# A transformer trunk on one core: first loads in smaller pieces over two queues, and three groups of work asked for later

## The chip, the cores and the metric

The kernel runs on one core of a Trainium2 chip. Its engines are named as the profile names them: PE (TensorE, the matmuls; PEld is its loading of weights), ACT (ScalarE), DVE (VectorE), POOL (GpSimd) and SP (SyncE, which issues most DMAs). Each takes its own list of instructions in order; semaphores hold an instruction until what it needs is there. The metric is the device time of one execution in microseconds (us).

## The reference

Two layers work on x, 256 positions of 1024 features. What matters here, cut from the reference:

```python
for l in range(DEPTH):                                   # DEPTH = 2
    x = x + 0.5 * swiglu(rmsnorm(x, ffn1_norm[l]), ffn1_w_gate[l], ffn1_w_up[l], ffn1_w_down[l])
    h = rmsnorm(x, mix_norm[l])
    proj = h @ w_in[l]                                   # q, k, v, xr, yr, cq and three gates
    ...
    br_attn = window_attention(q, k, v, attn_sinks[l]) @ w_attn_out[l]
    br_lru = rglru_branch(xr, yr, conv_w[l], conv_b[l], ...) @ w_lru_out[l]
    br_mem = memory_attention(cq, rmsnorm(mem, mem_norm[l]), w_mem_kv[l]) @ w_mem_out[l]
    merged = g[:, :, 0] * br_attn + g[:, :, 1] * br_lru + g[:, :, 2] * br_mem
    x = x + merged @ w_out[l]
    x = x + 0.5 * swiglu(rmsnorm(x, ffn2_norm[l]), ffn2_w_gate[l], ffn2_w_up[l], ffn2_w_down[l])
return rmsnorm(x, final_norm)
```

`rglru_branch` begins with a causal convolution of four taps along the positions, `xc[s] = conv_b + sum over d of conv_w[3-d] * xr[s-d]`; two gates come from products of `xc` with blocks of 64 x 64, through sigmoids.

## The kernel before

x lies feature-major in one buffer, eight tiles of 128 features x 256 positions. All weights were packed in the order of their use, in blocks of 128 x 128; eight blocks are a slab (128 x 1024 floats, 512 KB), 432 slabs in all. SP loads each slab into one of five stage buffers `st`. So that fp32 products can be made of fast ones, a slab is split: ACT makes the rounded high half `whi` (line 194), DVE the rest `wlo = st - whi` (line 195). Activations are split in the same way (`xs`, `h`, `xcs`). A block takes two matmuls: the high half against both halves of the activation, 512 columns (line 219), and the low half against the high one, 256 columns (line 220). The PSUM tiles of the pool `mm` have three buffers; each holds a pair of output tiles, and a later pair gets a buffer when the copies and sums that read it are done: ACT copies one half out, and one step later DVE adds the other (`join`, line 256).

The order of the lists is the order in which the Python code issues, and the code counts steps: when `block` (line 198) begins a slab, it first prepares slabs up to three ahead (`prep`: load, `whi`, `wlo`) and then calls `tick`, which runs all tasks that are due. `at(delay, f)` puts `f` into that list, `delay` slabs later. So a delay decides behind which other rows a task stands in the list of its engine, not when it runs.

`start` (line 384) issues nine warm-up matmuls on zeros, the loads of x (pairs of tiles), of the first five slabs and of the constants, then splits x times the norm's gain (`hi` on ACT or DVE at line 414 and 416, `lo` at line 324) and the first four slabs in pieces. The first norm needs the sum of squares over all features: ACT squares pairs of tiles (line 331), DVE adds them to `acc` (line 343), two matmuls `stat` against ones give the sums per position (line 284), nine small DVE rows make the reciprocal root `r` (lines 288 to 298), and two matmuls `rst` (line 305) spread it over the partitions. `n0.then(6, 8)` asks for `stat` at step 6 and `rst` at step 8. The first FFN products run on x without that factor, which is multiplied in later. `mem_norm` does the same for the memory tokens in layer 0: squares from step 5, `stat` and `rst` at steps 11 and 14 of its own count.

`mix` makes the projections pair by pair: `xr` (four pairs, tiles `pxr`), `kv` (`pkv`), q (`pq`, two pairs) and cq (`pcq`, two pairs), and behind each of the last four the products of the recurrent gates (`lg`, `lru_gates`). For each pair of `xr`, `conv` asks for the first tap on ACT (`first`, line 650, step 3), for the other three taps of each tile on DVE (`others`, line 654, steps 4 and 5) and for the split into `xcs` (ACT at step 6, DVE at step 7). The pairs are counted 0 to 3. `lru_gates` issues four sigmoids on ACT and the product `gi` on DVE (line 682). The first sigmoid behind other functions needs a table load.

Of the kernel before, what the change touches and what calls it, by code (L numbers as in the profile page):

```python
# [19 lines left out]
F32 = mybir.dt.float32  # L20
F32R = mybir.dt.float32r
I32 = mybir.dt.int32
AF = mybir.ActivationFunctionType
ALU = mybir.AluOpType
# [5 lines left out]
KT = D // 128  # L30
# [64 lines left out]
class Trunk:  # L95
# [288 lines left out]
    def start(self):  # L384
        nc = self.nc
        warm = self.sm("warm")
        nc.gpsimd.memset(warm, 1.0)
        nc.scalar.activation(warm, warm, AF.Silu)
        zero = self.s1("zero")
        nc.vector.memset(zero, 0.0)  # L390
        ps = self.att("warm")
        for _ in range(9):
            nc.tensor.matmul(ps[:, 0:128], zero[:, 0:128], zero[:, 128:256], start=True, stop=True)
        self.pk = self.pc.tile([128, NVEC], F32, name="pk")
        g = self.pk[:, 0:8]
        self.x = self.big("x")
        n0 = self.Norm(self, "ffn1_norm", 0)
        self.cst = self.pc.tile([128, 640], F32, name="cst")
        self.ones, self.ident, self.dist = self.cst[:, 0:128], self.cst[:, 128:256], self.cst[:, 256:640]
        ld = lambda p: nc.sync.dma_start(self.x[:, 2 * p:2 * p + 2, :], self.xT[:, 2 * p:2 * p + 2, :])  # L400
        ld(0)
        nc.scalar.dma_start(g, self.pkd[:, 0:8])
        for p in range(4):
            list(self.load(2))
            if p < 3:
                ld(p + 1)
        list(self.load())
        nc.sync.dma_start(self.cst, self.constd)
        nc.sync.dma_start(self.pk[:, 8:], self.pkd[:, 8:])

        for p in range(4):
            for k in (2 * p, 2 * p + 1):
                if k % 2:
                    nc.vector.tensor_scalar(n0.xs.hi(k), self.x[:, k, :], g[:, k:k + 1], None, op0=ALU.mult)
                else:
                    nc.scalar.activation(n0.xs.hi(k), self.x[:, k, :], AF.Copy, scale=g[:, k:k + 1])
            n0.lo_tiles(self.x, 2 * p, 2)
            list(self.prep(4 if p == 0 else 2))
        for p in range(4):
            self.at(1, n0.square, self.x, p)  # L420
            self.at(1 + p // 2, n0.add)
        n0.then(6, 8)
        return n0

# [47 lines left out]
    def mem_norm(self):  # L472

        n = self.Norm(self, "mem_norm", 0, split=False)
        self.load_mem()
        for p in range(4):
            self.at(5 + p, n.square, self.mem, p)
            self.at(6 + p, n.add)

        def b():  # L480
            self.Rm = self.pc.tile([128, 256], F32, name="Rm")
            self.rstd_b(n.r, self.Rm)

        self.at(11, n.a)
        self.at(14, b)

    def mem_split(self, l):
        m = self.mem
# [141 lines left out]
    def mix(self, l, norm, nxt):  # L630
        nc, V, A, G = self.nc, self.nc.vector, self.nc.scalar, self.nc.gpsimd
# [4 lines left out]
        xr, xc = self.big("xr"), self.big("xc")  # L636
        xcs = Halves(self, "xcs")

        def project(dst, ps):
            mult = lambda: V.tensor_tensor(dst, dst, norm.R2, op=ALU.mult)  # L640
            self.join(dst, ps, lambda: norm.when(mult))

        def conv(p, ps):
            project(xr[:, sl(p), :], ps)
            xq = slice(2 * p, 2 * p + 2)
            tap = lambda c, i: self.vec("conv_w", l, 8 * i + c)

            def first():
                for c in (2 * p, 2 * p + 1):
                    A.activation(xc[:, c, :], xr[:, c, :], AF.Identity, scale=tap(c, 3), bias=self.vec("conv_b", l, c))  # L650

            def others(c):
                for d in (1, 2, 3):
                    V.scalar_tensor_tensor(xc[:, c, d:], xr[:, c, :256 - d], tap(c, 3 - d), xc[:, c, d:],
                                           op0=ALU.mult, op1=ALU.add)

            self.at(3, first)
            self.at(4, others, 2 * p)
            self.at(5, others, 2 * p + 1)
            self.split(xc[:, xq, :], xcs, 2 * p, 2, delay=6)  # L660

        for p in range(4):
            conv(p, self.pair("pxr", w(C_XR, p), norm.xs))
# [42 lines left out]
        a, ms = self.big("a"), self.big("ms")  # L706
# [77 lines left out]
        for p in range(4):  # L784
            acc = None
            for nm, gt, X, n in (("w_attn_out", gates[0], out["A"], 4), ("w_mem_out", gates[2], out["C"], 4),
# [21 lines left out]
                acc = t  # L808
            if p < 3:
                self.split(acc, xm, 2 * p, 2, delay=2)  # L810
        n = self.Norm(self, *nxt)
        wo = lambda p: (lambda m: [("w_out", l, cols(128 * k), cols(128 * (2 * p + m))) for k in range(KT)])

        def add(p, ps):
            xp = self.x[:, sl(p), :]
            if p == 3:
                for m in range(2):
                    for i in range(2):
                        V.tensor_tensor(xp[:, m, :], ps[:, m, i, :], xp[:, m, :], op=ALU.add)
                    n.on_last(self.x, 6 + m)  # L820
                return
            for i in range(2):
                V.tensor_tensor(xp, ps[:, :, i, :], xp, op=ALU.add)
            n.on_pair(self.x, p)
# [7 lines left out]
    def attention_tasks(self, l, kv, vt, qcq, out):  # L832
# [124 lines left out]
        for qt, ts in enumerate(((16, 17, 19, 22), (19, 20, 22, 24))):  # L957
            for t, f in zip(ts, (mem_scores, mem_exp, mem_norm, mem_transpose)):
                self.at(t, f, qt)
# [97 lines left out]
```

## Time and profile before

| what | us |
|---|---|
| three runs of the kernel | 1281.79, 1282.45, 1290.47 |
| their median | 1282.45 |
| the profiled execution, its own time | 1282.87 |
| its span, from the first to the last instruction | 1281.1 |
| PE busy in the span | 1265.4 (99%) |
| DVE busy | 985.7 (77%) |
| ACT busy | 761.3 (59%) |
| moved by DMA | 232.40 MB, 181 GB/s |

The times of single rows come from the profiled execution. Its own time is 1.8 us more than its span, for what lies before the first instruction and behind the last. A matmul counts as busy until its modelled end, so that two that follow each other without a pause overlap; the same holds for ACT and DVE rows, whose next row starts about 0.1 us before the one ahead of it has ended. A wait that the profile names after an engine is put down to the semaphore that came last by its records.

### The profile page before, as it was taken

What the parts mean: (1) busy time and instruction counts of PE and PEld (TensorE: products, weight loads), DVE (VectorE), ACT (ScalarE), POOL (GpSimd) and SP (SyncE); (2) the same over time, 40 slices, a digit from 0 to 9 for tenths busy, and PEclk for the clock granted to TensorE, in tenths of its full rate; (3) what the DMA queues carried; (4) which work ended last, traced back from release to release, by engine and by line L of the source; (5) the groups of instructions that cost most, each with busy time, mean ns of one, the idle gap of its engine ahead of it and who ended that gap; (6) DMA issues with size and microseconds to landing.
All of it is one profiled execution on the core that took longest, in us unless ns stands there. A gap on an engine that the chain in (4) does not pass through costs nothing.

```text
span 1281.1 us, 19099 instructions
## 1 busy us (share of the span) xinstructions
PE 1265.4 (99%) x7318; PEld 1104.4 (86%) x7318; DVE 985.7 (77%) x1406; ACT 761.3 (59%) x1134; POOL 0.3 (0%) x5
## 2 busy tenths in 40 slices
PE   8999999999999999999999999999999999999997
PEld 7888888888888888888888888888888888888886
DVE  7788766888789987677678775669887898876754
ACT  5656544588577565555456564447867675655542
POOL 0000000000000000000000000000000000000000
PEclk9999999999999999999999999999999999999998
DMA  8665665555445566666656665564554465665651
GB/s 288 209 189 167 214 183 179 172 175 166 144 131 187 187 197 189 195 187 202 194 184 208 189 188 195 167 204 156 183 165 132 148 199 180 197 195 185 195 184 48
DMA packets 64748, 232.40 MB, mean 181 GB/s; under 512 B 7313, under 2 KB 7441, under 8 KB 64401
## 3 DMA queue, kind: packets, MB, share of 16 engines
q1 hardware_dynamic: 64224, 230.65, 57.2%
q8 instruction: 58, 0.95, 0.3%
q10 hardware_dynamic: 432, 0.53, 0.1%
q14 instruction: 34, 0.27, 0.1%
HBM read 230.10 MB, written 1.05 MB: 180 GB/s over the span
## 4 chain that ended last, share of the span: by engine, by line
PE 90%; DVE 5%; ACT 3%; issue 1%; DMA 1%; SPq 0%; DVEq 0%; ACTq 0%
PE pd L219 12%; PE pg L219 11%; PE pu L219 11%; PE pd L220 6%; PE pgt L219 6%; PE pu L220 6%; PE pg L220 6%; PE pbr L219 5%; PE pgt L220 3%; DVE wlo L195 2%; PE pyr L219 2%; PE pwo L219 2%; PE pbr L220 2%; PE pxr L219 2%; PE pgu L219 2%; PE pcq L219 1%
## 5 line engine op out<-in xcount | busy, mean ns | idle before, releaser
L195 DVE TENSOR_TENSOR wlo<-st,whi 128x1024 fp32r<-128x1024 f32 (+2 forms) x438 | 524.6, 1206 | 238.1 <-ACT whi L194 238.0
L194 ACT ACTIVATE whi<-st 128x1024 fp32r<-128x1024 f32 (+2 forms) x438 | 443.5, 1045 | 39.5 <-PE pd L219 20.5
L219 PE MATMUL pd<-h,whi 128*128 128x512 f32 x660 | 230.1, 393 | 0.0
L219 PE MATMUL pg<-xs,whi 128*128 128x512 f32 x640 | 225.2, 394 | 0.0
L219 PE MATMUL pu<-xs,whi 128*128 128x512 f32 x640 | 225.1, 393 | 0.0
L220 PE MATMUL pd<-h,wlo 128*128 128x256 f32 x660 | 184.9, 280 | 0.0
L220 PE MATMUL pg<-xs,wlo 128*128 128x256 f32 x640 | 179.3, 280 | 0.8 <-DVE wlo L195 0.8
L220 PE MATMUL pu<-xs,wlo 128*128 128x256 f32 x640 | 179.3, 280 | 0.0
L219 PEld LDWEIGHTS pd<-h,whi 128*128 128x128 f32 x660 | 123.6, 187 | 28.1
L219 PEld LDWEIGHTS pg<-xs,whi 128*128 128x128 f32 x640 | 119.9, 187 | 27.0
L219 PEld LDWEIGHTS pu<-xs,whi 128*128 128x128 f32 x640 | 119.8, 187 | 26.9
L219 PE MATMUL pgt<-xs,whi 128*128 128x512 f32 x384 | 139.2, 405 | 0.0
L220 PEld LDWEIGHTS pd<-h,wlo 128*128 128x128 f32 x660 | 124.7, 189 | 0.0
L220 PEld LDWEIGHTS pg<-xs,wlo 128*128 128x128 f32 x640 | 120.9, 189 | 1.1 <-DVE wlo L195 1.1
L220 PEld LDWEIGHTS pu<-xs,wlo 128*128 128x128 f32 x640 | 121.0, 189 | 0.0
L220 PE MATMUL pgt<-xs,wlo 128*128 128x256 f32 x384 | 107.6, 280 | 0.0
L219 PEld LDWEIGHTS pgt<-xs,whi 128*128 128x128 f32 x384 | 72.1, 188 | 19.5 <-issue 3.0
L258 ACT COPY g<-pg 128x512 f32<-128x512 f32 x40 | 23.5, 586 | 99.7 <-PE pg L220 92.9
L220 PEld LDWEIGHTS pgt<-xs,wlo 128*128 128x128 f32 x384 | 72.5, 189 | 0.2
L270 ACT ACTIVATE h<-u 128x512 fp32r<-128x512 f32 x44 | 27.8, 632 | 46.2 <-DVE u L523 43.9
L320 ACT ACTIVATE xs<-x,pk 128x256 fp32r<-128x256 f32 x40 | 18.7, 503 | 49.2 <-DVE x L559 21.6
L219 PE MATMUL pgu<-xs,whi 128*128 128x512 f32 x128 | 44.7, 394 | 1.2 <-DVE xs L324 1.2
(237 smaller groups left out, 2053.5 us busy)
## 6 DMA issues: line engine op xcount, KB each, us to landing
st<-wpack SPq DMA_DIRECT2D x428, 512.0 KB, 3.8
st<-wpack SPq DMA_DIRECT2D x8, 256.0 KB, 4.9
mem<-memT SPq DMA_DIRECT2D x2, 1024.0 KB, 6.7
x<-xT SPq DMA_DIRECT2D x4, 256.0 KB, 5.0
outT<-xg SPq DMA_DIRECT2D x2, 256.0 KB, 2.6
outT<-xg ACTq DMA_DIRECT2D x2, 256.0 KB, 2.7
cst<-cst SPq DMA_DIRECT2D x1, 320.0 KB, 7.8
pk<-pk SPq DMA_DIRECT2D x1, 128.0 KB, 7.5
```

The costliest lines, as they stand in the source:

```text
L194: nc.scalar.activation(hi[:, c], st[:, c], AF.Copy)
L195: nc.vector.tensor_tensor(lo[:, c], st[:, c], hi[:, c].bitcast(F32), op=ALU.subtract)
L219: mm(both, hi, X.both(k), start=(k == 0), stop=False)
L220: mm(out[:, 0, :], lo, X.hi(k), start=False, stop=(k == n - 1))
L258: self.nc.scalar.copy(dst, ps[:, :, 1, :])
L270: hi = lambda: self.nc.scalar.activation(X.hi(k, n), src, AF.Copy)
L320: self.t.nc.scalar.activation(self.xs.hi(k), x[:, k, :], AF.Copy, scale=self.t.vec(self.v, self.l, k))
```

## The change

Four edits, two of them in `start`:
- The loads: tile 0 of x alone on SP's queue, tile 1 on ACT's queue behind the gains of the norm, the first slab in four pieces, then the other pairs of x, each ahead of its slab in two pieces as before. The splitting of x goes tile by tile, between the pieces of the slabs; `hi` of tiles 0, 3 and 7 is DVE's, of the others ACT's.
- The squares of x are asked for at steps 2 and 3 in place of 1; the sums are three over pairs of tiles (128 x 512, line 431 of the new kernel) and one over the two halves (line 434), at steps 3 to 4 in place of 1 to 2.
- `stat` and `rst` of the memory's norm one step later, 12 and 15.
- In `conv`, all tasks of pairs 2 and 3 later, by 1 and 2 steps.

```diff
-        ld = lambda p: nc.sync.dma_start(self.x[:, 2 * p:2 * p + 2, :], self.xT[:, 2 * p:2 * p + 2, :])
-        ld(0)
+        ld = lambda e, a, b: e.dma_start(self.x[:, a:b, :], self.xT[:, a:b, :])
+        ld(nc.sync, 0, 1)
         nc.scalar.dma_start(g, self.pkd[:, 0:8])
-        for p in range(4):
+        ld(nc.scalar, 1, 2)
+        list(self.load(4))
+        for p in range(1, 4):
+            ld(nc.sync, 2 * p, 2 * p + 2)
             list(self.load(2))
-            if p < 3:
-                ld(p + 1)
         list(self.load())
         nc.sync.dma_start(self.cst, self.constd)
         nc.sync.dma_start(self.pk[:, 8:], self.pkd[:, 8:])
 
+        for k in range(KT):
+            if k == 0 or k % 4 == 3:
+                nc.vector.tensor_scalar(n0.xs.hi(k), self.x[:, k, :], g[:, k:k + 1], None, op0=ALU.mult)
+            else:
+                nc.scalar.activation(n0.xs.hi(k), self.x[:, k, :], AF.Copy, scale=g[:, k:k + 1])
+            if k % 2 == 0:
+                parts = self.prep(4 if k == 0 else 2)
+            if k == 1:
+                next(parts)
+            n0.lo_tiles(self.x, k, 1)
+            for _ in range(2 if k == 0 else 1):
+                next(parts)
+        list(parts)
         for p in range(4):
-            for k in (2 * p, 2 * p + 1):
-                if k % 2:
-                    nc.vector.tensor_scalar(n0.xs.hi(k), self.x[:, k, :], g[:, k:k + 1], None, op0=ALU.mult)
-                else:
-                    nc.scalar.activation(n0.xs.hi(k), self.x[:, k, :], AF.Copy, scale=g[:, k:k + 1])
-            n0.lo_tiles(self.x, 2 * p, 2)
-            list(self.prep(4 if p == 0 else 2))
-        for p in range(4):
-            self.at(1, n0.square, self.x, p)
-            self.at(1 + p // 2, n0.add)
+            self.at(2 + p // 2, n0.square, self.x, p)
+
+        def add(i):
+            a = n0.sq[0]
+            if i < 4:
+                nc.vector.tensor_tensor(a, a, n0.sq[i], op=ALU.add)
+                return
+            n0.acc = self.ps1.tile([128, 256], F32, tag="acc", name=self.name("acc"), bufs=1)
+            nc.vector.tensor_tensor(n0.acc, a[:, 0, :], a[:, 1, :], op=ALU.add)
+
+        for i in range(1, 5):
+            self.at(2 + (i + 1) // 2, add, i)
         n0.then(6, 8)
...
-        self.at(11, n.a)
-        self.at(14, b)
+        self.at(12, n.a)
+        self.at(15, b)
...
-            self.at(3, first)
-            self.at(4, others, 2 * p)
-            self.at(5, others, 2 * p + 1)
-            self.split(xc[:, xq, :], xcs, 2 * p, 2, delay=6)
+            late = (0, 0, 1, 2)[p]
+            self.at(3 + late, first)
+            self.at(4 + late, others, 2 * p)
+            self.at(5 + late, others, 2 * p + 1)
+            self.split(xc[:, xq, :], xcs, 2 * p, 2, delay=6 + late)
```

What the edits make of the lists, at three places. In the names the first number behind `whi`, `wlo` and `st` is the slab, counted from 0; other numbers tell buffers apart.

DVE, around the sum of squares of the first norm, before:

```order
L343 TENSOR_TENSOR acc_29_188<-acc_29_188,sq_30_190 128x256 x2
L195 TENSOR_TENSOR wlo_4_217<-st_4_124,whi_4_216 128x1024
L343 TENSOR_TENSOR acc_29_188<-acc_29_188,sq_31_194 128x256 x2
L343 TENSOR_TENSOR acc_29_188<-acc_29_188,sq_32_196 128x256 x2
L195 TENSOR_TENSOR wlo_5_243<-st_5_146,whi_5_242 128x1024
L195 TENSOR_TENSOR wlo_6_265<-st_6_158,whi_6_264 128x1024
```

The same place on DVE now:

```order
L195 TENSOR_TENSOR wlo_4_208<-st_4_127,whi_4_207 128x1024
L195 TENSOR_TENSOR wlo_5_234<-st_5_147,whi_5_233 128x1024
L431 TENSOR_TENSOR sq_28_211<-sq_28_211,sq_29_213 128x512
L431 TENSOR_TENSOR sq_28_211<-sq_28_211,sq_30_237 128x512
L195 TENSOR_TENSOR wlo_6_262<-st_6_159,whi_6_261 128x1024
L431 TENSOR_TENSOR sq_28_211<-sq_28_211,sq_31_239 128x512
L434 TENSOR_TENSOR acc_32_266<-sq_28_211 128x256
```

The last sum, `acc`, stood ahead of the low halves of slabs 5 and 6 and now stands behind both. On PE the matmuls `stat` that read it stand where they stood, behind the last block of slab 4 and ahead of slab 5:

```order
L219 MATMUL pg_37_288<-xs_6_105,whi_4_207 128x512
L220 MATMUL pg_37_288<-xs_6_105,wlo_4_208 128x256
L284 MATMUL stat_38_319<-cst_106,acc_32_266 128x1 x2
L219 MATMUL pg_37_288<-xs_5_104,whi_5_233 128x512
L220 MATMUL pg_37_288<-xs_5_104,wlo_5_234 128x256
```

That row of PE has only other buffer numbers than before.

ACT in `mix` of layer 0, from the split of pair 1 (`xcs_232`) on, before (`xc` are first taps, `xcs_233` the split of pair 2, and the row with `r` the first sigmoid of `lg_272`):

```order
L270 ACTIVATE xcs_232_2161<-xc_231_2160 128x2x256
L258 COPY kv_264_2369<-pkv_265_2370 128x512
L194 ACTIVATE whi_87_2433<-st_87_2311 128x1024
L650 ACTIVATE xc_231_2160<-xr_230_2159,pk_102 128x256 x2
L194 ACTIVATE whi_88_2463<-st_88_2340 128x1024
L270 ACTIVATE xcs_233_2162<-xc_231_2160 128x2x256
L258 COPY qcq_269_2429<-pq_270_2430 128x512
L194 ACTIVATE whi_89_2491<-st_89_2371 128x1024
L680 ACT_TABLE_LOAD
L680 ACTIVATE r_263_2368<-lg_272_2488,pk_102 128x256
```

ACT at the same place now:

```order
L270 ACTIVATE xcs_232_2161<-xc_231_2160 128x2x256
L666 ACTIVATE xc_231_2160<-xr_230_2159,pk_102 128x256 x2
L258 COPY kv_264_2369<-pkv_265_2370 128x512
L194 ACTIVATE whi_87_2430<-st_87_2311 128x1024
L194 ACTIVATE whi_88_2458<-st_88_2340 128x1024
L258 COPY qcq_269_2426<-pq_270_2427 128x512
L194 ACTIVATE whi_89_2485<-st_89_2371 128x1024
L270 ACTIVATE xcs_233_2162<-xc_231_2160 128x2x256
L666 ACTIVATE xc_231_2160<-xr_230_2159,pk_102 128x256 x2
L697 ACT_TABLE_LOAD
L697 ACTIVATE r_263_2368<-lg_272_2482,pk_102 128x256
```

The first taps of pair 2 moved ahead of the copy of `kv` and of `whi_87`; the split of pair 2 and the first taps of pair 3 (the second `xc` row) now stand directly ahead of the table load and the sigmoids.

DVE in the same stretch, from the product `gi` of the first gates (`lg_272`) to the sum of the second q pair (`pq_273`), before:

```order
L682 TENSOR_TENSOR gi_262_2367<-gi_262_2367,xc_231_2160 128x512
L195 TENSOR_TENSOR wlo_90_2530<-st_90_2401,whi_90_2529 128x1024
L195 TENSOR_TENSOR wlo_91_2557<-st_91_2431,whi_91_2556 128x1024
L271 TENSOR_TENSOR xcs_233_2162<-xc_231_2160,xcs_233_2162 128x2x256
L682 TENSOR_TENSOR gi_262_2367<-gi_262_2367,xc_231_2160 128x512
L195 TENSOR_TENSOR wlo_92_2592<-st_92_2461,whi_92_2591 128x1024
L261 TENSOR_TENSOR qcq_269_2429<-pq_273_2518,qcq_269_2429 128x512
```

Now:

```order
L699 TENSOR_TENSOR gi_262_2367<-gi_262_2367,xc_231_2160 128x512
L195 TENSOR_TENSOR wlo_90_2523<-st_90_2399,whi_90_2522 128x1024
L271 TENSOR_TENSOR xcs_233_2162<-xc_231_2160,xcs_233_2162 128x2x256
...
L195 TENSOR_TENSOR wlo_91_2553<-st_91_2428,whi_91_2552 128x1024
...
L699 TENSOR_TENSOR gi_262_2367<-gi_262_2367,xc_231_2160 128x512
L195 TENSOR_TENSOR wlo_92_2590<-st_92_2456,whi_92_2589 128x1024
L261 TENSOR_TENSOR qcq_269_2426<-pq_273_2511,qcq_269_2426 128x512
```

At each "..." stand the three rows of `others` for one tile of pair 3; before, both stood further up. The second `pcq` pair takes the PSUM buffer that the last of these rows frees.

## Rows read from the trace of the kernel before

**Rows 1.** PE's waits: engine, line, released by, total us, times, longest.
```profile
PE pq L219 <- ACT xcs L270: 1.5, 2, 0.8
PE pgu L219 <- DVE xs L324: 1.2, 1, 1.2
PE pg L220 <- DVE wlo L195: 0.8, 1, 0.8
...
PE stat L284 <- DVE acc L343: 0.5, 1, 0.5
```
**Rows 2.** Timeline, ACT: start and length in us, row, [idle before, releaser].
```profile
14.49 2.18 ACT L331 ACTIVATE sq<-x 128x512 f32<-128x512 f32 x4
...
17.80 1.06 ACT L194 ACTIVATE whi<-st 128x1024 fp32r<-128x1024 f32 x1 [0.18 <-DMA st<-wpack]
```
**Rows 3.** Timeline, DVE, behind the sum of squares.
```profile
24.51 0.68 DVE L261 TENSOR_TENSOR u<-pgu,u 128x512 f32<-128x512 f32 x1
25.11 1.22 DVE L195 TENSOR_TENSOR wlo<-st,whi 128x1024 fp32r<-128x1024 f32 x1
26.24 0.15 DVE L288 TENSOR_SCALAR v<-stat 128x2 f32<-128x2 f32 x1
```
**Rows 4.** Timeline, PE, first block behind `stat`, and `rst`.
```profile
21.98 0.48 PE L219 MATMUL pg<-xs,whi 128*128 128x512 f32 x1
...
28.62 0.71 PE L305 MATMUL rst<-cst,r 128*128 128x128 f32 x4 [0.84 <-DVE r L298]
```
**Rows 5.** Timeline, PE in `mix` of layer 0: second `pq`, both `pcq`.
```profile
256.89 0.47 PE L219 MATMUL pq<-xs,whi 128*128 128x512 f32 x1 [0.76 <-ACT xcs L270]
...
264.17 0.40 PE L219 MATMUL pcq<-xs,whi 128*128 128x512 f32 x1
...
271.26 0.40 PE L219 MATMUL pcq<-xs,whi 128*128 128x512 f32 x1
```
**Rows 6.** Timeline, DVE in the same stretch.
```profile
248.99 0.68 DVE L261 TENSOR_TENSOR xr<-pxr,xr 128x512 f32<-128x512 f32 x1
...
250.32 1.22 DVE L195 TENSOR_TENSOR wlo<-st,whi 128x1024 fp32r<-128x1024 f32 x1
251.46 1.51 DVE L654 SCALAR_TENSOR_TENSOR xc<-xr,pk,xc 128x255 f32<-128x255 f32 x3
...
256.06 0.68 DVE L261 TENSOR_TENSOR kv<-pkv,kv 128x512 f32<-128x512 f32 x1
...
269.67 0.68 DVE L261 TENSOR_TENSOR qcq<-pq,qcq 128x512 f32<-128x512 f32 x1
```
**Rows 7.** Timeline, ACT in the same stretch.
```profile
249.17 0.63 ACT L270 ACTIVATE xcs<-xc 128x512 fp32r<-128x512 f32 x1 [2.28 <-DVE xc L654]
...
250.18 1.06 ACT L194 ACTIVATE whi<-st 128x1024 fp32r<-128x1024 f32 x1
251.13 1.08 ACT L650 ACTIVATE xc<-xr,pk 128x256 f32<-128x256 f32 x2
...
258.32 1.28 ACT L680 ACT_TABLE_LOAD   x1
259.61 0.47 ACT L680 ACTIVATE r<-lg,pk 128x256 f32<-128x256 f32 x1
...
261.05 1.07 ACT L194 ACTIVATE whi<-st 128x1024 fp32r<-128x1024 f32 x1
```
**Rows 8.** Stretch at the end: its us, PE busy (x), PEclk, DMA, GB/s.
```profile
1274.00:1276.00 2.00, 0.73 (x4) 0.51 0.00 0
```
**Rows 9.** Warm-up matmuls before 3.5 us and behind 4.4: busy us, mean ns.
```profile
L393 PE MATMUL warm<-zero 128*128 128x128 f32 x11 | 2.7, 436 | 1.2 <-DVE zero L390 1.2
L393 PE MATMUL warm<-zero 128*128 128x128 f32 x5 | 0.8, 292 | 0.0
```
**Rows 10.** Two stretches of FFN work: us, PE busy (x), PEclk, DMA, GB/s.
```profile
80.00:200.00 120.00, 120.00 (x681) 1.00 0.62 192
480.00:640.00 160.00, 160.00 (x925) 1.00 0.62 193
```

## The prediction, made before the changed kernel ran

> **What bounds the kernel now.** The page first: PE (TensorE) is busy 99% of the span, so a change can win little but PE's remaining waits, and lose by making new ones. PE's own waits come next: those in the parts that this change touches are short, 1.2 us before the first real matmul, 0.8 us for the low half of a weight slab, 0.5 us for the statistic's input, and twice 0.8 us at `pq`, once in each layer [rows 1]. About 5 us with the wait at 28.62 [rows 4], 0.4% of the time; the rest of PE's idle time is the end of the kernel. The third look is at the engines that feed PE at these places, in order of time. VectorE (DVE) and ScalarE (ACT) run their lists strictly in order, so each place is read as a chain: which row of which engine has to end before PE may go on. Two such chains carry the forecast, the statistic of the first norm (rows 2 to 4) and the convolution of the recurrent branch (rows 5 to 7).
>
> **Which time the sum is made against.** The profiled execution took 1282.87 us, 0.4 us over the median of 1282.45. I add the terms to the first and take 0.4 off.
>
> **First loads.** The first tile of x comes alone, the first slab in four pieces, tile 1 over ACT's queue. PE can start earlier, at best by the 1.2 us that it waited [rows 1]; I take some 0.4, with 0 and 1.2 as ends. Moving the squares behind slab 4's high half lets `whi_4` and `wlo_4` follow the load at once, so the 0.8 us wait of `pg` goes too. Both gains lie ahead of the statistic's matmul, and what PE wins there it may lose again at it, as follows.
>
> **Squares and sums of the first norm.** In the order of PE nothing moves: the two `stat` matmuls stand between slab 4 and slab 5. In DVE's order the last sum (`acc`) stood ahead of `wlo_5`; now it stands behind `wlo_5` and `wlo_6` (the order piece in the text above). That is a wait added on PE, with all later matmuls queued behind it. When does `acc` end? `whi_5` began at 17.80 as its slab landed [rows 2], a transfer that keeps its place and its bytes. With 1.06 us for it, `wlo_5` starts at 18.90; a slab's low half keeps DVE 1.13 us (25.11 to 26.24) and a 128x512 sum 0.60 (24.51 to 25.11) [rows 3], 0.72 where the next row needs its result (two such rows fill 248.99 to 250.32 [rows 6]). So: first sum 20.03, second 20.75, `wlo_6` 21.35, third sum 22.48, `acc` 23.20, and its end, with 0.42 for half the width, at 23.62. ACT keeps up: two squares of 0.55 [rows 2] and `whi_6` behind `whi_5` end near 20.9. PE then needs about 0.5 for the `stat` matmuls: next slab at 24.1, where before it came at 21.98 [rows 4]. That is 2.1 us later than before, whatever the start won; the early gains cost nothing and bring nothing.
>
> Part of it returns. Before, PE stood 0.84 us at `rst` for the reciprocal root [rows 4], about 1.0 with the restart. Behind `acc` DVE still has `wlo_7`, two sums, `wlo_8` (3.5 us) and the chain from `v` to `r`, 2.4 us (26.24 to 28.62) [rows 3, 4]: it ends near 29.4, and PE, moved by 2.1, is there at 29.7. No wait: the 1.0 goes. Term: +1.1 us, between 0.5 and 1.6, for landings half a us to either side.
>
> **Statistic of the memory one step later.** A step is a slab, 8 blocks of PE. The 0.5 us wait [rows 1] goes, with 0.2 for the restart: -0.7. Its reader, `rst`, moves one step with it, so the spacing stays, and DVE has only one more `wlo` and two 0.6 us rows ahead of the chain: no new wait. Ends: -0.8 and 0.
>
> **Convolutions of the third and fourth pairs later.** The wait at 256.89 is named after ACT's `xcs` [rows 5], but by the program this matmul wants the PSUM buffer that `kv`'s sum on DVE frees; that sum starts at 256.06 and lasts 0.68 [rows 6], so it ends at 256.74, just ahead of the matmul. Taking three convolution rows out from in front of it helps; but ACT's list is changed too. I follow both from the point to which they are equal (on the clock of before).
> ACT: `xcs` of pair 1 at 249.17; a row of ACT starts 0.1 before the one ahead of it ends (250.18 and 1.06 against 251.13) [rows 7]. Now the first taps of pair 2 come next (249.7, 1.0 for the two), then the copy of `kv` (0.5), then `whi_87`, which before began at 250.18: now 251.2 to 252.2.
> DVE: the sum of `xr` at 248.99, `wlo_86` at 250.32, free at 251.46 [rows 6]; it then idles until `whi_87` ends. `wlo_87` 252.3, `xcs` 253.4, one convolution from 254.0 (1.51 for its three rows [rows 6], 1.43 to the next), `kv`'s sum 255.4 to 256.1. PE's `pq` starts at 256.3 instead of 256.89: 0.6 won.
> DVE goes on with `kv` scaled, `wlo_88` and the second convolution of pair 2, which ends at 259.4. Now ACT's `xcs` of pair 2 waits for that convolution, and behind it in ACT's list stand the first taps of pair 3, the table load and the four sigmoids of the first gates. Before, the table load began at 258.32, the sigmoids at 259.61, and they were through for the next row at 261.05 [rows 7]. Now: `xcs` 259.5, taps 260.05, table 261.15, sigmoids 262.45 to 264.0.
> PE's `pcq` needs the PSUM buffer that the last sigmoid frees: 256.3 + 7.28 (256.89 to 264.17 [rows 5]) would be 263.55, so it waits until 264.1. The 0.6 us are gone.
> DVE stands before the `gi` product from 261.8 to 264.0, as that needs the sigmoids. Then `gi` (0.6), `wlo_90` (its `whi_90` ends at 264.95), `xcs`, convolution, `wlo_91`, convolution, `gi`, `wlo_92`: 265.0 + 1.14 + 0.6 + 1.43 + 1.14 + 1.43 + 0.6 + 1.14 = 272.5, and only then `qcq`'s sum, until 273.15. Before it stood at 269.67 [rows 6]. The second `pcq` wants the buffer that this sum frees. PE would be there at 264.1 + 7.1 = 271.2 (264.17 to 271.26 [rows 5]) and starts at 273.3: 2.0 us later than in the kernel before, after a wait of 2.1.
> Both layers have this order: +4.1 us. Ends: each layer 0.8 faster (the old wait gone, no new one) to 3 slower (every row of the chain 5% longer).
>
> **A rule on the clock.** The profile grants PE the full clock all the way but at the end, where PE is busy 0.73 us of 2 and the granted share falls to 0.51, the lower level of 1.2 GHz [rows 8]. The new wait at `stat` empties PE for over 3 us (20.4 to 23.7). The Trainium skill, TensorE: Matmul & The Clock Gate, section "HAM oscillation — how this bites in real kernels", says that PE waiting for data between bursts can lose its clock, so that the next burst starts cold. By that rule the restart behind `stat` would run at the lower level; the trace shows such a fall only in the thin work at the end. I do not put it into the sum.
>
> **Sum.** 1282.87 + 1.1 - 0.7 + 4.1 = 1287.4, less 0.4: **1287.0 us**, 0.4% slower.
>
> **Rivals.**
> 1. *The convolutions do what they are moved for, and the kernel is not slower.* The place is `qcq`'s sum ahead of the second `pcq`. For it: DVE's rows alone, without idle time, would reach it at 269.9 and end at 270.6, ahead of PE's 271.2. Against: two idle stretches of DVE, 0.8 and 2.2 us, that ACT's list makes. It decides where the sum ends before 271.1, that is if the sigmoids come at least 2.1 us earlier than I have them. Price: 0.8 won in each layer instead of 2.0 lost: 1287.0 - 5.6 = 1281.4.
> 2. *The start stays won*: `acc` is there when PE comes. For it: fewer and wider sums. Against: two slabs' low halves in front of it. Then 0.4 + 0.8 + 1.0 are gained in place of +1.1: 1283.7.
> 3. *The clock falls in the wait at `stat`.* The warm matmuls of the start take 436 ns within the first 3.5 us and 292 behind 4.4 [rows 9], so about 3 us of dense work passed before the rise. Such a stretch at half speed costs 1.5 us: 1288.5. For it: a wait this long is new; against: nothing in the middle of the run has shown it.
> 4. *PE's pace changes.* Equal work runs at two paces: 681 matmuls in 120 us, but 925 in 160 [rows 10], that is 176 and 173 ns each, 1.9% apart at the full clock in both. If a changed restart moves a stretch of some 180 us to the other pace, the time moves by 3.4: 1283.6 or 1290.4.
>
> **How the numbers follow.** Forecast 0.54, rival 1 0.14, rival 2 0.10, rival 3 0.12, rival 4 0.10, half to each side. The range 1282.0 to 1290.5 holds all of them but most of rival 1 and the ends of rival 4. A measurement tells about 1% from no change here, 12.8 us, since one of the three runs of before was 8 us over the others. All cases lie inside it. Slower by more would need several stretches to change pace or waits double mine (0.05), faster by more has not enough idle time to win (0.01), within 1% 0.94.
>
> **What would show it.** In the trace of the changed kernel: PE waits over 3 us at `stat` for DVE's `acc`, ending near 23.7, and none at the first `rst`; no wait for the memory's statistic; two waits near 2 us at `pcq`, one in each layer, with DVE idle before the `gi` product for ACT. The forecast is wrong if `stat` does not wait, or if no wait of PE in the mixing stage is over 1 us.

## The result, and the profile after

The changed kernel is 0.55% slower: 1289.07 us (median of 18 runs, 1287.05 to 1296.59) against 1282.32 for the kernel before (18 runs, 1280.67 to 1290.47); ratio 1.0055, 95% interval 1.0042 to 1.0068. The forecast was 1287.0, so its direction holds and 2.1 us are missing.

The profiled execution took 1296.59 us (span 1294.7), far over its median, and that has to be understood before any row of it is read. The view of stretches, with the columns of [rows 8] (stretch; its us; busy time of PE, PEld, DVE, ACT, POOL with the number of instructions; PEclk; DMA; GB/s):

```profile
80.00:200.00 120.00, 120.00 (x696) 105.83 (x695) 92.69 (x142) 66.82 (x90) 0.00 (x0) 1.00 0.60 195
480.00:640.00 160.00, 160.00 (x907) 138.69 (x906) 110.11 (x129) 87.01 (x112) 0.00 (x0) 1.00 0.61 188
24.55:27.69 3.14, 3.14 (x11) 2.66 (x11) 3.09 (x6) 0.00 (x0) 0.00 (x0) 0.50 0.74 245
27.90:31.00 3.10, 3.10 (x19) 2.68 (x19) 1.71 (x10) 1.84 (x3) 0.00 (x0) 1.00 0.67 209
273.90:277.00 3.10, 3.10 (x12) 2.62 (x11) 3.10 (x4) 3.10 (x6) 0.00 (x0) 0.51 0.69 230
912.60:915.70 3.10, 3.10 (x18) 2.68 (x19) 3.10 (x4) 3.10 (x7) 0.00 (x0) 1.00 0.67 193
```

The first two rows are the two paces of [rows 10] with the places exchanged: 681 matmuls became 696 between 80 and 200, and 925 became 907 between 480 and 640, both at the full clock. In the trace the starts of successive blocks lie 346.7 or 353.3 ns apart, and PE stays in the one or the other for up to 180 us. Here three long stretches behind 400 us went at the slower pace. So that traces can be compared, I take this part out: for every two successive blocks less than 0.4 us apart, what lies over 346.7 ns. That is 7.2 us in the trace of before and 13.1 in that of after. What is left is 1273.85 and 1281.63, a difference of 7.8 us, and it can be followed from mark to mark (after less before, in us, the slow-pace part taken out of both; the second trace of the changed kernel is the run `after_2` below):

| up to | after, first trace | after, second trace |
|---|---|---|
| first real matmul | -1.1 | -1.2 |
| slab 5 on PE, behind `stat` | +2.4 | +1.8 |
| first `rst` | +2.9 | +2.4 |
| keys of the memory, layer 0 (`mk`) | +2.0 | +1.5 |
| first `pyr`, layer 0 (behind both `pcq`) | +5.6 | +3.5 |
| first `pq`, layer 1 | +5.6 | +3.6 |
| first `pyr`, layer 1 | +7.6 | +5.6 |
| end of the span | +7.8 | +6.0 |

So time is lost at two kinds of place, the start and the two mixing stages, and next to none elsewhere (0.2 and 0.4 us behind the last of them). PE's waits name them (engine, line, released by, total us, times, longest):

```profile
PE pcq L219 <- DVE qcq L261: 3.6, 2, 1.8
PE stat L284 <- DVE acc L434: 1.8, 1, 1.8
...
PE pgu L219 <- ACT whi L194: 1.1, 1, 1.1
PE pcq L219 <- ACT gi L698: 0.6, 2, 0.3
```

Against [rows 1], the waits at `pq`, at `wlo` and at the memory's `stat` are gone, as is the first one at `rst`; `stat` of the first norm, `pcq` and the high half of slab 1 (`pgu` for `whi`) are new. At the start, DVE's timeline (start, length, row, [idle before, releaser]):

```profile
19.12 1.23 DVE L195 TENSOR_TENSOR wlo<-st,whi 128x1024 fp32r<-128x1024 f32 x1 [1.32 <-ACT whi L194]
20.26 1.48 DVE L431 TENSOR_TENSOR sq<-sq,sq 128x512 f32<-128x512 f32 x2
21.66 1.22 DVE L195 TENSOR_TENSOR wlo<-st,whi 128x1024 fp32r<-128x1024 f32 x1
22.79 0.68 DVE L431 TENSOR_TENSOR sq<-sq,sq 128x512 f32<-128x512 f32 x1
23.51 0.43 DVE L434 TENSOR_TENSOR acc<-sq 128x256 f32<-128x256 f32 x1
```

and PE's:

```profile
21.95 0.28 PE L220 MATMUL pg<-xs,wlo 128*128 128x256 f32 x1
23.99 0.70 PE L284 MATMUL stat<-cst,acc 128*128 128x1 f32 x4 [1.76 <-DVE acc L434]
24.55 0.78 PE L219 MATMUL pg<-xs,whi 128*128 128x512 f32 x1
...
25.34 0.63 PE L219 MATMUL pg<-xs,whi 128*128 128x512 f32 x1
...
31.75 0.60 PE L305 MATMUL rst<-cst,r 128*128 128x128 f32 x4
```

`acc` ends at 23.94, behind `wlo_5` and `wlo_6` as the order has it. Behind the wait a block's first matmul takes 0.63 us where it took 0.40, and the third row of the first view says why: granted share 0.50, the 1.2 GHz level, until about 27.8, then 1.00. `rst`, the last row, waits for nothing.

In the mixing stage of layer 0, ACT:

```profile
259.26 0.64 ACT L270 ACTIVATE xcs<-xc 128x512 fp32r<-128x512 f32 x1 [3.21 <-DVE xc L670]
259.80 1.08 ACT L666 ACTIVATE xc<-xr,pk 128x256 f32<-128x256 f32 x2
260.90 1.28 ACT L697 ACT_TABLE_LOAD   x1
...
263.28 0.48 ACT L698 ACTIVATE gi<-lg,pk 128x256 f32<-128x256 f32 x1
```

DVE:

```profile
263.80 0.69 DVE L699 TENSOR_TENSOR gi<-gi,xc 128x512 f32<-128x512 f32 x1 [2.16 <-ACT gi L698]
...
272.23 0.68 DVE L261 TENSOR_TENSOR qcq<-pq,qcq 128x512 f32<-128x512 f32 x1
```

and PE:

```profile
263.81 0.50 PE L219 MATMUL pcq<-xs,whi 128*128 128x512 f32 x1 [0.33 <-ACT gi L698]
...
272.96 0.50 PE L219 MATMUL pcq<-xs,whi 128*128 128x512 f32 x1 [1.79 <-DVE qcq L261]
```

ACT stood 3.2 us for DVE's convolution with the sigmoids queued behind it; DVE then stood 2.2 us for the sigmoids; the sum that frees the PSUM buffer ended at 272.91, and the second `pcq` began then, 9.15 us behind the first where it was 7.09 [rows 5]. Behind that wait, from 273.9 to 277.0, the granted share is 0.51 once more. In layer 1 the same wait has the full clock behind it (912.6 to 915.7).

### The profile page after: what moved, and what is told of

Same layout as the page of the kernel before. It is cut to its first block, busy times and chain, and to the rows that moved or that the text cites. A ratio compares the mean times of both kernels' runs of the same rounds, so it can differ in the third digit from the quotient of the medians.

```text
span 1294.7 us, 19109 instructions
## 1 busy us (share of the span) xinstructions
PE 1276.4 (99%) x7318; PEld 1109.7 (86%) x7318; DVE 986.0 (76%) x1402; ACT 761.5 (59%) x1135; POOL 0.3 (0%) x5
## 4 chain that ended last, share of the span: by engine, by line
PE 89%; DVE 5%; ACT 3%; DMA 1%; issue 1%; SPq 0%; DVEq 0%; ACTq 0%
PE pd L219 12%; PE pu L219 11%; PE pg L219 11%; PE pd L220 6%; PE pu L220 6%; PE pg L220 6%; PE pgt L219 6%; PE pbr L219 5%; PE pgt L220 3%; PE pyr L219 2%; PE pbr L220 2%; PE pwo L219 2%; DVE wlo L195 2%; PE pxr L219 2%; PE pgu L219 2%; ACT whi L194 1%
## 5 line engine op out<-in xcount | busy, mean ns | idle before, releaser
L219 PE MATMUL pg<-xs,whi 128*128 128x512 f32 x640 | 228.1, 398 | 0.0
L270 ACT ACTIVATE h<-u 128x512 fp32r<-128x512 f32 x44 | 27.8, 632 | 48.0 <-DVE u L539 45.6
```

What stands on the lines that cost most here:

```text
L219: mm(both, hi, X.both(k), start=(k == 0), stop=False)
L270: hi = lambda: self.nc.scalar.activation(X.hi(k, n), src, AF.Copy)
```

## The experiments

The theory was the forecast's two chains, and a third part that the trace had just shown: the clock falls behind a wait of almost 2 us, at some 1.5 us each time. The rivals lay the whole loss on one end, or the slow blocks on something else than the clock. "Pace-free" below is a span with the slow-pace part taken out as above, less that of the kernel before (1273.85; a second trace of it lies 0.6 lower). A "fall" is a stretch at the lower clock behind a wait.

### The convolutions alone, traced three times

The kernel before with only the last edit:

```diff
+            late = (0, 0, 1, 2)[p]
-            self.at(3, first)
+            self.at(3 + late, first)
...
-            self.split(xc[:, xq, :], xcs, 2 * p, 2, delay=6)
+            self.split(xc[:, xq, :], xcs, 2 * p, 2, delay=6 + late)
```

> The kernel before with one edit: all tasks of the convolutions of pairs 2 and 3 later by 1 and 2 steps. Theory (ACT's list delays the sigmoids, these delay DVE, and the second pcq waits for the sum on DVE): PE waits about 0.3 and 1.8 us at pcq in each layer, none at pq, net +1.9 us a layer; behind a wait that long the granted clock may fall to the lower level as it did once in the changed kernel, +1.4 us each time. Time 1286.2 us with no fall, 1287.6 with one, 1289.0 with two, against 1282.3 before. Rival (the loss is all at the start, the convolutions cost nothing): 1281 to 1282.5 us and no wait at pcq.

> A second trace of the kernel before with only the convolution delays, whose 12 times went from 1285.3 to 1301.0 us. Theory: the waits at pcq are again 0.3 and 1.9 us in each layer, to 0.1 us, and what lies over 1285.3 is made of blocks at the slower pace (353 ns in place of 347) and of blocks at the lower clock behind the pcq waits, so that the span less these two parts agrees with the first trace within 0.5 us. Rival (the waits themselves vary from run to run): they differ by 1 us or more.

> A third trace of the same kernel; the same is expected of it.

Measured: median 1291.64 us (12 runs) against 1283.60 for the kernel before on the same chip, ratio 1.0064 (1.0040 to 1.0087). The first trace is of the fastest of these runs, 1285.26; PE's waits in it:

```profile
PE pcq L219 <- DVE qcq L261: 3.7, 2, 1.9
...
PE pcq L219 <- ACT gi L682: 0.6, 2, 0.3
```

No wait at `pq` is left. The waits are the same in the other two traces (3.6 and 0.6 or 0.7), and each mixing stage gave one of two sums: +2.0 and +2.1 us pace-free in the first trace, +3.6 and +3.6 in the second, +2.0 and +3.6 in the third. The granted clock tells them apart. First trace, 3.1 us behind the two waits:

```profile
270.80:273.90 3.10, 3.10 (x20) 2.68 (x19) 3.10 (x4) 3.10 (x6) 0.00 (x0) 1.00 0.69 234
902.00:905.10 3.10, 3.10 (x20) 2.68 (x19) 3.10 (x4) 3.10 (x6) 0.00 (x0) 1.00 0.72 217
```

Second trace:

```profile
273.90:277.00 3.10, 3.10 (x12) 2.62 (x11) 3.07 (x5) 2.80 (x5) 0.00 (x0) 0.50 0.69 241
905.30:908.40 3.10, 3.10 (x11) 2.62 (x11) 3.07 (x5) 2.77 (x5) 0.00 (x0) 0.50 0.73 244
```

So the mechanism costs 2.0 us a layer, and the clock behind it 0 or 1.6. The three traced runs took 1285.26, 1289.10 and 1287.32 us, with no, two and one fall; their slow-pace parts are alike (6.3 to 6.7). The rival with a free convolution falls. The median of this kernel is higher than any traced run of it, its slowest run took 1301.0, and its median lies 8.0 us over before where the whole change costs 6.75; what those runs hold was not traced, so it stays open.

### The start alone

The changed kernel with `late = 0`:

```diff
-            late = (0, 0, 1, 2)[p]
+            late = 0
```

> The changed kernel with the delays of the convolutions taken back (loads, squares and memory statistic stay as changed). Theory: what is left is the start, +2.6 us where slab 5 begins on PE, +1.4 for the low clock behind that wait, less 1.0 for the wait at rst and 1.1 for the memory's statistic: 1284.2 us, with the stat wait of 1.8 us, four or five blocks at 0.64 us behind it, and pq waiting 0.8 us in each layer again. Rival (all of the loss is in the convolutions): 1281.5 us.

Measured: median 1283.94 us, ratio 1.0009 (0.9986 to 1.0032), that is, no difference to be told. Its trace has the wait at `stat`, 2.0 us, and behind it the lower clock, for nine blocks this time (the `stat` rows; the eleventh block behind them; a stretch between):

```profile
23.81 0.93 PE L284 MATMUL stat<-cst,acc 128*128 128x1 f32 x4 [1.98 <-DVE acc L434]
...
30.98 0.40 PE L219 MATMUL pu<-xs,whi 128*128 128x512 f32 x1
```

```profile
24.40:27.60 3.20, 3.20 (x11) 2.81 (x12) 3.13 (x7) 0.00 (x0) 0.00 (x0) 0.50 0.73 246
```

Pace-free it is 4.0 us over before. Eight full blocks of 0.64 us in place of 0.347 make 2.3 of it; the `stat` rows and the first block ran at the lower clock too, and the next run shows what the fall cost in all. `pq` waits 0.8 us in each layer again, and `pcq` does not. With the run before it this settles that the loss has two places, and that most of what a measurement sees is the convolutions.

### Keeping PE busy in the wait

As the last one, with 14 matmuls of 256 columns ahead of `stat`, read by nobody:

```diff
+        def fill():
+            ps = self.att("fill")
+            for _ in range(14):
+                nc.tensor.matmul(ps[:, 0:256], n0.xs.hi(0)[:, 0:128], n0.xs.hi(1), start=True, stop=True)
+
+        self.at(6, fill)
         n0.then(6, 8)
```

> As the run without the convolution delays, with 14 idle matmuls of 256 columns on PE ahead of the first stat (their result is read by nobody), which fill some 1.7 us of its wait. Theory (the slow blocks behind the wait are the granted clock, which falls because PE stood empty): the wait still ends near 24.0 us, no block behind it takes 0.64 us, the granted share stays at 1, and the time is 1.4 us below the run without the fill, about 1282.8 us. Rival (the blocks are slow for another reason, as DVE, ACT or the loads at that place): the slow blocks stay, and so does the time, 1284.2 us or more.

Measured: median 1283.56 us, ratio 1.0007 (0.9991 to 1.0023). The medians of the two runs are too alike to tell them apart (1.4 us were expected, 0.4 seen, while each spreads over 8 us or more), but the traces do. PE, then the same stretch as above:

```profile
21.49 1.84 PE L442 MATMUL fill<-xs 128*128 128x256 f32 x14
23.93 0.58 PE L284 MATMUL stat<-cst,acc 128*128 128x1 f32 x4 [0.60 <-PE fill L442]
...
27.92 0.39 PE L219 MATMUL pu<-xs,whi 128*128 128x512 f32 x1
```

```profile
24.40:27.60 3.20, 3.20 (x20) 2.81 (x21) 3.13 (x6) 0.13 (x1) 0.00 (x0) 1.00 0.80 259
```

`stat` starts when it did, at 23.9, so nothing was won at the wait itself; but 20 matmuls in place of 11 fit into the next 3.2 us, with the same loads and the same work on DVE. From the start of `stat` to the eleventh block (the last row of the first view) it is 4.0 us where it was 7.2, so the fall had cost 3.2. Pace-free the kernel is 0.6 over before, 3.4 less than without the fill. The slow blocks are the clock, and the clock fell because PE stood empty.

### The split behind the sigmoids

The changed kernel, with ACT's and DVE's split of pair 2 one step later:

```diff
-            self.split(xc[:, xq, :], xcs, 2 * p, 2, delay=6 + late)
+            self.split(xc[:, xq, :], xcs, 2 * p, 2, delay=6 + late + (p == 2))
```

> The changed kernel with the split of pair 2 into xcs one step later again, so that on ACT it stands behind the four sigmoids of the first gates and not ahead of them. Theory (the sigmoids are held up by that split, which waits for DVE's convolution): the sigmoids end near 260.5 instead of 263.8 on the changed kernel's clock, DVE has no idle time ahead of gi, the qcq sum ends near 270.2, no wait over 0.3 us is left at pcq, and pq stays without its wait: 1289.1 - 2 x 2.1 - 1.4 for the clock = 1283.5 us. Rival (DVE has too many rows ahead of that sum, whatever ACT does): the second pcq still waits over 1 us in each layer, 1287 to 1289 us.

Measured: median 1284.98 us (1283.5 was expected), ratio 1.0011 (0.9988 to 1.0035); the loss at the start, 3.1 us up to `mk` in its trace, is still in it. In that trace (0.85 us later than the changed kernel's at this place) the last sigmoid on ACT:

```profile
260.28 0.49 ACT L698 ACTIVATE gi<-lg,pk 128x256 f32<-128x256 f32 x1
```

and on DVE:

```profile
262.40 0.69 DVE L699 TENSOR_TENSOR gi<-gi,xc 128x512 f32<-128x512 f32 x1
...
270.47 0.68 DVE L261 TENSOR_TENSOR qcq<-pq,qcq 128x512 f32<-128x512 f32 x1
```

The sigmoids end at 260.77, on the changed kernel's clock 3.8 us earlier; DVE has no idle time ahead of `gi`; the sum ends at 271.15 (270.3 on the changed kernel's clock); and PE waits neither at `pcq` nor at `pq`. The mixing stages now win 0.6 us each against before, pace-free, instead of losing 2.0 or 3.6. One row on ACT made the loss; the number of rows on DVE did not, as the same eight, from the first `gi` on, stand ahead of the sum in both kernels.

### The sums early, and both mends together

The run with `late = 0`, with other steps for squares and sums:

```diff
-            self.at(2 + p // 2, n0.square, self.x, p)
+            self.at(2 + p // 3, n0.square, self.x, p)
...
-            self.at(2 + (i + 1) // 2, add, i)
+            self.at(2 + i // 3, add, i)
```

> The run without the convolution delays, with three of the four squares at step 2 (the fourth at 3), and the sums at steps 2, 2, 3 and 3: on DVE two of them stand behind wlo_4, where DVE was idle for 1.3 us, and acc stands ahead of wlo_6 again. Theory (stat waits because acc stands behind wlo_6): acc ends near 21.6 us, PE does not wait at stat by more than 0.2 us, the clock stays full, rst may wait up to 1 us as in the kernel before; with the slow-pace part taken out of the spans it is 4 us below the run without the convolution delays and 1.5 to 2 below the kernel before; median about 1281. Rival (the smaller first loads leave the engines behind in any order): stat still waits over 1 us and the time is that of the run without the convolution delays, 1283.9.

The second kernel has this and the split behind the sigmoids.

> Both mends together: sums early as in the run beside this one, convolutions late as in the change but the split of pair 2 behind the first sigmoids. Theory: no wait at stat, pq or pcq over 0.3 us, a further 0.7 us won in each layer at pq: with the slow-pace part taken out of the spans 3 us below the kernel before, median about 1279.5. Rival (what is won at pq is given back at the next wait): the span without the slow-pace part equals that of the run beside it within 0.5 us.

Measured: 1281.53 us with the sums early, ratio 0.9994 (0.9986 to 1.0002), no difference to be told; 1278.19 with both (8 runs), ratio 0.9977 (0.9965 to 0.9988), each against 1282.39 on the same chip. DVE and PE of the first:

```profile
18.26 1.48 DVE L431 TENSOR_TENSOR sq<-sq,sq 128x512 f32<-128x512 f32 x2
19.66 1.22 DVE L195 TENSOR_TENSOR wlo<-st,whi 128x1024 fp32r<-128x1024 f32 x1
...
21.51 0.42 DVE L434 TENSOR_TENSOR acc<-sq 128x256 f32<-128x256 f32 x1
```

```profile
22.07 0.53 PE L284 MATMUL stat<-cst,acc 128*128 128x1 f32 x4
...
28.89 0.71 PE L305 MATMUL rst<-cst,r 128*128 128x128 f32 x4 [0.64 <-DVE r L298]
```

`stat` has no wait, and no block behind it is at the lower clock. But pace-free only 0.7 us are won, not 1.5 to 2: PE starts 1.1 us earlier and then stands for slab 1 (the `pgu` wait for `whi`, 0.4 to 1.2 us in every trace with the new loads), and `rst` waits again, so that at `rst` it is level with before; the 0.7 are the memory's statistic. The smaller first loads by themselves won nothing. With both mends PE's waits are down to

```profile
PE rst L305 <- DVE r L298: 1.5, 2, 1.3
...
PE pgu L219 <- ACT whi L194: 1.2, 1, 1.2
...
PE wt L906 <- ACT P L939: 0.4, 2, 0.2
```

and pace-free it is 2.6 us under before, 0.6 of it in each mixing stage. It beats both kernels, and the rival (given back at the next wait) falls.

### Single edits, and second traces

The kernel before with only the memory's statistic a step later:

```diff
-        self.at(11, n.a)
-        self.at(14, b)
+        self.at(12, n.a)
+        self.at(15, b)
```

> The kernel before with only the memory's statistic one step later. Theory: PE's wait of 0.5 us at that stat is gone, rst for it does not wait, 0.7 to 1.1 us won there on PE. Rival (the chain to r becomes late): PE waits at that rst.

Measured: 1282.27 us in one run. The wait is gone, the memory's `rst` has none, and between the first `rst` and `mk` the kernel wins 0.8 us pace-free (from -0.35 to -1.1).

The kernel before with only the new squares and sums, at steps 2 and 3, and 3 to 4, as in the change:

```diff
-            self.at(1, n0.square, self.x, p)
-            self.at(1 + p // 2, n0.add)
+            self.at(2 + p // 2, n0.square, self.x, p)
...
+            self.at(2 + (i + 1) // 2, add, i)
```

> The kernel before with only the squares and sums of the first norm as changed (loads as before). Theory (it is the place of acc behind wlo_6 on DVE, not the loads): the wait of 0.8 us for wlo at pg is gone, PE waits about 2 us at stat, the next slab begins near 24.1 us, and the granted clock may fall behind it (1.4 to 2.4 us). Rival (the new loads bring the wait): stat waits under 0.5 us.

Measured: 1280.78 us in one run; PE:

```profile
22.97 0.61 PE L284 MATMUL stat<-cst,acc 128*128 128x1 f32 x4 [0.60 <-DVE acc L428]
```

This lies between the theory and its rival. `acc` ends at 22.91, 2.3 us later than in the kernel before (20.59), so its place does make it late. But in this run slab 5 landed about 1 us sooner than in the changed kernel (`whi_5` at 17.01 against 18.02), and PE came late, since its first blocks, 7.5 to 10.1 us, took 0.64 us each, as they do at the lower clock. The wait was 0.6 us where 2 were expected, and the clock stayed full behind it. The loads account for part of the rest: where ACT waited for slab 5 to land, `whi_5` began between 16.67 and 17.80 in the seven traces with the old loads (17.1 in the mean) and between 17.41 and 18.02 in five with the new (17.7). So of the 1.8 us at `stat` I put some 0.6 down to the new loads and the larger part to the sums' place; that is an estimate from these landings, as no run has the new loads with the old sums.

> A second trace of the changed kernel. Theory: stat waits 1.8 to 2.0 us and the clock falls behind it, the waits at pcq are 0.3 and 1.8 us in each layer; the span less the slow-pace part lies within 1.5 us of the first trace's (a fall of the clock more or less). Rival: the long waits are not there in a run near the median of 1289.1.

Measured: 1296.01 us in one run. The waits that were named are the same to 0.1 us (`stat` 1.8, `pcq` 3.7 and 0.6 over both layers). The clock fell behind `stat` and behind neither `pcq`: pace-free 1.8 under the first trace (1.5 was allowed), which had one such fall more. Its slow-pace part is 14.3 us, 13.1 in the first trace; in the traces of the other kernels it lies between 5 and 10.

> A second trace of the kernel before. Theory: the span less the slow-pace part is within 0.5 us of the first trace's, with the slow pace in other stretches; no block in the middle of the run at the lower clock. Rival: the waits differ from the first trace's by 1 us or more.

Measured: 1281.75 us. Pace-free 0.6 under the first trace (0.5 was allowed). It comes from the start: slab 5 began 0.74 us sooner and the first `rst` 1.3, as that wait was not there; behind 30 us the waits are those of the first trace but for 0.3 us more at the memory's `stat`.

## Why the prediction was right, and where it fell short

**Convolutions, +2.0 us a layer: right, in each step.** Forecast and first trace of after, on clocks that agree to some 0.3 us: sigmoids end 264.0, 263.76; first `pcq` 264.1, 263.81; `qcq`'s sum ends 273.15, 272.91; second `pcq` 273.3, 272.96. Where the clock did not fall a stage cost 2.0 to 2.1 us in six cases of six. Rival 1 falls, and with the point from which I had it decide: taking the split away from in front of the sigmoids brought them 3.8 us earlier (2.1 were needed), and the stage then wins 0.6 us, near the 0.8 of the rival's price.

**First norm, +1.1 us: right in the chain, near in sum, and one of its steps mis-sized.** `acc` was to end at 23.62 and did at 23.94; the next slab was to start at 24.1 and did at 24.55; the wait at `rst` went, as the chain ended at 29.64 (29.4) ahead of PE. With the clock kept up by the fill, `rst` stands +1.2 us against before. That it came so near is in part luck: of the six traces with the old start and the old sums, the one that I worked from reaches `rst` last, pace-free 0.1 to 1.3 us behind the others, and against the mean of the six the term measures 1.8, over its upper end of 1.6. What failed is the wait's length, over 3 us in the forecast and 1.8 in the trace: I had PE at `stat` at 20.4, but it came at 22.2. It started 1.1 us earlier (I had 0.4) and then stood 1.1 us for the high half of slab 1, which I had not looked for. As `acc` decides when PE goes on, this changed nothing in the sum. The 23.62 was near also by luck: I let slab 5 land at 17.80, as "a transfer that keeps its place and its bytes", but it lands some 0.6 us later with the new loads, and 17.80 was the latest of the old ones. Rival 2 falls.

**Memory, -0.7 us: right.** 0.8 measured with that edit alone.

**The clock, left out of the sum: this is the step that failed.** I wrote "I do not put it into the sum", and gave rival 3 a chance of 0.12, as nothing in the middle of the run had shown a fall. In the four traces with the long wait at `stat` (1.8 to 2.0 us) the clock fell each time, for five to nine blocks. From the start of `stat` to the eleventh block behind it took 5.6 us in both traces of the changed kernel and 7.2 in the other two, where the fill had 4.0: a fall cost 1.6 or 3.2 us, and the price of 1.5 was right for the low end. The Trainium skill, TensorE: Matmul & The Clock Gate, section "HAM oscillation — how this bites in real kernels", describes a kernel whose PE waits for data between bursts of matmuls and starts the next burst cold. Its waits are longer than these; here 1.8 us was enough, and the wait of over 3 us that I had forecast was a reason to put the price into the sum. Second, I looked at one wait only. The clock also fell behind the second `pcq`, in four of ten cases, at 1.4 to 1.6 us each.

The sum with these put in: 1287.0, and 1.5 at `stat`, and 0.4 of two falls of 1.5, 1.2, make 1289.7; the measured median is 1289.07. This lies in the stated range, whose upper end was drawn for such a case.

**Pace, rival 4.** It makes the traced runs of the changed kernel slow, and by what can be inferred it does not part the medians. The two traces of the changed kernel have 13.1 and 14.3 us of it, and took over 1296 us; but its median of 1289.07, less 1.9 outside the span and less the mean of its two spans without the slow-pace part, 1280.7, leaves 6.4 us. For the kernel before the same (1282.32 - 1.8 - 1273.6) gives 6.9. No run at the median of the changed kernel was traced, so this is not shown, and the reckoning does not hold everywhere: for the convolutions alone it leaves over 10 us, where the three traces have 6.3 to 6.7.

## What to carry to other kernels

A task that is asked for later is not only late itself: on an engine that takes its list in order it becomes the row that stands in front of others. Before delaying work, look at what is queued behind each row that moves, and on whom that row waits; here one split of 0.6 us, put ahead of four sigmoids, cost 2 us a layer, and putting it behind them turned a loss into a gain.

A wait on TensorE has two prices, its length and what the clock does behind it; where a forecast makes a new wait of almost 2 us in dense work, reckon with 1.5 to 3 us more (it came in eight of fourteen cases here), and if the wait can't be removed, matmuls that nobody reads can keep the clock, as 14 of them did here.

## What the runs showed of the hardware that was not expected

- A wait of 1.8 us in dense matmul work was enough to bring the granted clock down to 1.2 GHz for five to nine blocks, in four of four cases at `stat` and four of ten at the second `pcq`. Waits up to 0.9 us between 11 us and the end of the dense work were never followed by a fall. What decides in the cases between is open: the waits at `pcq` are alike to 0.1 us in traces with and without a fall.
- At the start the first blocks ran at the lower clock in three of seven traces with the old loads (three to five full blocks of 0.64 us, 0.9 to 1.5 us in all). No trace shows that the clock had risen before them and fell: in all three the 18 warm-up matmuls took 4.21 us, the length of the lower clock to their end, where the first trace of before, whose clock rose within them, has 3.74. In the second trace of the convolutions alone:

```profile
1.18 4.21 PE L393 MATMUL warm<-zero 128*128 128x128 f32 x18 [1.18 <-DVE zero L390]
...
7.34 0.63 PE L219 MATMUL pgu<-xs,whi 128*128 128x512 f32 x1
```

  The granted share reads 1.00 there all the same, so in the first 10 us the length of the matmuls tells the clock and that column does not.
- PE has two paces at the full clock, 346.7 and 353.3 ns for a block of two matmuls. It keeps one for up to 180 us and changes only where something interrupts the blocks. The slow-pace part lay between 4.9 and 14.3 us in the 14 traces; two traces of one kernel differed in it by at most 1.2 us, and that untraced runs of the changed kernel have some 7 us less is inferred from medians. Without that part taken out, changes of a few us can't be told from single traces.
